# A two-layer attention backbone: a unit's maxes turned by two small matmuls on their way to their row, and output stores entering the queue one batch later

## The chip, the cores and the metric

The kernel runs on one core of one Trainium2 chip. The metric is the device time of one execution in microseconds (us). A core has a matrix engine (TensorE, "PE" in the profile, with its weight loads as "PEld"), a vector engine (VectorE, "DVE"), an engine for functions of one operand (ScalarE, "ACT"), a general engine (GpSimd, "POOL") and SyncE ("SP"), which in this kernel issues every DMA, in the order of the program. PE writes its results to PSUM, from where DVE and ACT read them; everything else lies in SBUF, and DRAM is reached by DMA alone.

## The reference

Two layers over 2048 latent tokens and 256 context tokens of width 1024. In each layer a modulated RMS norm feeds one input projection; its columns go to latent attention (6 heads, "MLA"), to grouped-query attention (6 heads on 2 key heads, "GQA") and to a convolution; their outputs are gated, joined and mapped by one output projection. What bears on the change is the attention:

```python
def block_attention(q, k, v):
    ...
    def one_block(qi):
        s = jnp.einsum('bqgrd,bkgd->bgrqk', qi, k).astype(jnp.float32) * scale
        p = jax.nn.softmax(s, axis=-1).astype(v.dtype)
        return jnp.einsum('bgrqk,bkgv->bqgrv', p, v)
    ...
o_mla = block_attention(q_mla, jnp.concatenate([k_mla, k_mla_c], axis=1),
                        jnp.concatenate([v_mla, v_mla_c], axis=1))
o_gqa = block_attention(q_gqa, jnp.concatenate([k_gqa, k_gqa_c], axis=1),
                        jnp.concatenate([v_gqa, v_gqa_c], axis=1))
```

Latent queries see all 2304 keys; in the first layer the 256 context queries see the context keys alone. In the last layer there are no context queries.

## The kernel before

The program is a row of stages: `projections(0)`, `attention(0)`, `projections(1)` (which ends layer 0 with its output projection and begins layer 1), `attention(1)`, and a last `projections(2)`. The change lies in `attention`. In the profile, attention of layer 0 runs from about 795 to 2070 us, that of layer 1 from about 2935 to 4180 us.

**Units and steps.** A unit is one head and one chunk of queries: chunks 0 to 3 have 512 latent queries, chunk 4 the 256 context queries (layer 0 alone). Heads run in the order 6 to 11 (GQA), then 0 to 5 (MLA). A unit of 512 queries has nine steps, each over 256 keys; a context unit has one. So layer 0 has 6 + 6 heads of 37 steps, layer 1 of 36 steps, and there are 106 units besides the first of each layer, 12 of them context units.

**One step** is a turn of the loop at lines 1605 to 1632. `rows_step` moves the rows of maxes on (below). `s_pair` multiplies the keys with the queries into a PSUM tile `s` (four pairs of matmuls for GQA, five for MLA; the last one adds the row of maxes, which lies in a row of the query tile `qd`), and ACT takes the exponential into a buffer `p`. `next(stream)` does one step of the maxes of a later unit. `sums` adds the buffers on POOL. When enough steps are pending, a batch of them is multiplied with the values (`pv_pair`, PSUM tile `o`): five at a unit's sixth step, four at the next unit's first step (three at a time in the last head). After a unit's last product ACT copies `o` to a tile `e` and SP is given the two stores of it. `finish` makes the sums over keys of two units at a time, copies them to another `e` tile of the same pool of two buffers and gives SP the stores `sm`; their reciprocals are then loaded, computed and stored by tasks of the next stage's planner.

**The maxes.** `max_stream` runs ahead of the units by LEAD steps. For a unit it multiplies queries (as the stationary operand) with a part of the keys into PSUM tiles `m` (a pool of three buffers), eight steps of 512 keys and one of the rest, and DVE reduces each to a column of `mx`, and `mx` to `nm`: 128 partitions x 4 columns, one column for each 128 queries, negated. The matmuls need this as a row of 512 on one partition. Lines 1421 to 1432 do that by DRAM: a step after `nm` is there, the store `nm<-nm` writes it with rows and columns exchanged, and three steps later two loads `qd<-nm` put the row into partitions 32 and 96 of `qd`.

```python
if r[0] == ROW_IN:
    dma(row.rearrange("(j p) -> p j", p=128), r[2].bitcast(F32))
elif r[0] == 0:
    for o, i in m_parts(u, qt[u], row):
        dma(out=o, in_=i)
```

**The order of SP's queue** is that in which `dma` is called. When `max_stream` begins a unit it also calls for the queries of the unit after it (4 DMAs for GQA, 10 for MLA; in chunk 3 those of two units). At the third step of a head's first chunk the next head's keys and values are called for (`load_kv`: `big<-kn` four times, `big<-vm`; for the first MLA head the shared rotary keys as well). The row of the first unit of a layer is made in the projections (`first_unit`, lines 1249 to 1291).

Of the kernel before, what the change touches and what calls it, by code (L numbers as in the profile page):

```python
# [9 lines left out]
F32 = mybir.dt.float32  # L10
F32R = mybir.dt.float32r
# [276 lines left out]
def hybrid_dit(ctx: ExitStack, tc: tile.TileContext, I: dict, out: bass.AP):  # L288
# [1080 lines left out]
    def attention(l, out_proj):  # L1369
        z = scratch[l]  # L1370
        with ExitStack() as ps_:
# [45 lines left out]
                    dma(out=o, in_=i)  # L1417

            rows_due = []

            def rows_step():
                for r in rows_due:
                    r[0] -= 1
                    h, c = u = r[1]
                    row = z.nm[h, c]
                    if r[0] == ROW_IN:
                        dma(row.rearrange("(j p) -> p j", p=128), r[2].bitcast(F32))
                    elif r[0] == 0:
                        for o, i in m_parts(u, qt[u], row):
                            dma(out=o, in_=i)  # L1430
                while rows_due and rows_due[0][0] <= 0:
                    rows_due.pop(0)
# [3 lines left out]
            def max_stream():  # L1436
                for i, u in enumerate(units[1:], 1):
                    h, c = u
                    n = CH[c][1] // 128
                    ahead = i + 2 if c == 3 else i + 1  # L1440
                    while loaded[0] < min(ahead, len(units) - 1):
                        loaded[0] += 1
                        load_q(units[loaded[0]])
                    a, _, cr, _ = qt[u]
                    k = kH[kv_id(h) % 2]
                    mx = mp.tile([128, 4, 6], F32, tag="mx", name="mx")
                    nm = mp.tile([128, 4], F32R, tag="nm", name="nm")
                    ops = [(a, k)] + ([(cr, kR)] if h < MH else [])

                    def banks():  # L1450
                        return [p_m.tile([128, 512], F32, tag="m", name="m") for _ in range(2)]

                    def scores(ps, q, o, w, at=0):
                        for i, (x, y) in enumerate(ops):
                            for e in range(2):
                                r = slice(64 * e, 64 * e + 64)
                                T.matmul(out=ps[e][:, at:at + w], lhsT=x[r, q * 128:q * 128 + 128], rhs=y[r, o:o + w],
                                         start=(i == 0), stop=(i == len(ops) - 1))

                    if c < 4:  # L1460
                        for q in range(n):
                            for i in range(2):
                                ps = banks()
                                scores(ps, q, i * 512, 512)
                                for e in range(2):
                                    V.tensor_reduce(out=mx[:, q, 2 * i + e:2 * i + e + 1], in_=ps[e], op=ALU.max,
                                                    axis=AX.X)
                                yield
                    ps = banks()
                    for q in range(n):  # L1470
                        scores(ps, q, NK - 128, 128, q * 128)
                    for e in range(2):
                        V.tensor_reduce(out=mx[:, 0:n, 4 + e], in_=ps[e][:, 0:n * 128].rearrange("p (q k) -> p q k", k=128),
                                        op=ALU.max, axis=AX.X)
                    V.tensor_reduce(out=nm[:, 0:n], in_=mx[:, 0:n, 0 if c < 4 else 4:6], op=ALU.max, axis=AX.X,
                                    negate=True)
                    rows_due.append([ROW_IN + 1, u, nm[:, 0:n]])
                    yield

            st = {}  # L1480
# [51 lines left out]
            def pv_pair(u, j, t, N, p):  # L1532
# [9 lines left out]
                if j == N - 1:  # L1542
# [6 lines left out]
                    A.activation(out=e1, in_=s["o"], func=AF.Copy)  # L1549
                    r = slice((h % 2) * 64, (h % 2) * 64 + 64)  # L1550
                    o = z.o[h // 2, c]
                    dma(out=o[0, r, :], in_=e1[0:64, :])
                    dma(out=o[1, r, :], in_=e1[64:128, :])
                    fin.append(u)

            fin, ended = [], []

            def finish(last=False):

# [2 lines left out]
                while fin:  # L1562
# [11 lines left out]
                    for e, u in enumerate(us):  # L1574
                        h, c = u
                        fin.remove(u)
                        st.pop(u)
                        dma(out=z.sm[c][h:h + 1, :], in_=e2[64 * e:64 * e + 1, :])
                        out_proj.sch.add(1, out_proj.recip(h, c))

            LAG = 1
            ROW_IN = 3
            LEAD = 16
            qt[units[0]], qt[units[1]] = qall[0:2]
            o, i = kv_parts(z, 0)[-1]
            dma(out=o, in_=i)
# [18 lines left out]
            for u, j, t, N in steps:  # L1605
# [12 lines left out]
                sums(u, j, p, N)  # L1618
                pend.append((u, j, t, N, p))
                if len(pend) >= LAG + batch(pend):  # L1620
                    finish()
                    if pend[0][3] > 1:
                        folds += ended
# [9 lines left out]
            while pend:  # L1633
                finish()
                for x in [pend.pop(0) for _ in range(batch(pend))]:
                    pv_pair(*x)
            folds += ended
            fold_step()
            finish(True)

    stage = [projections(l) for l in range(DEPTH + 1)]
    for _ in stage[0]:
# [89 lines left out]
```

## Time and profile before

| | |
|---|---|
| median of 3 runs | 4395.1 us (4394.66 to 4397.02) |
| the profiled execution | 4391.08 us |
| its span, first to last instruction | 4389.3 us |
| mean granted TensorE clock over the span | 0.946 |
| PE busy | 4012.7 us (91%) |
| DVE busy | 2501.8 us (57%) |
| ACT busy | 1892.2 us (43%) |
| POOL busy | 2478.5 us (56%) |

A row of the waits names the engine that waits, what it waits for, and then us in total, times, and the longest. A row of the timeline has start, duration, engine, line, operation, output <- inputs, shapes and count; in brackets stands how long its engine had been idle, and what ended that. Buffer numbers are left out of names. Almost every instruction has line 159, where a helper records it, so names tell more than lines; SP's DMAs of attention have line 1366, those of the planner line 244. A row of the stretches of time has start and end, length, busy us (and instructions) of PE, PEld, DVE, ACT and POOL, then PE's granted clock, the busy share of the DMA engines, and GB/s.

### The profile page before, as it was taken

To read this page: it belongs to the slowest core of one execution; us is meant where nothing else is said; L and a number is where in the kernel's file an instruction comes from. 1 tells how busy PE (TensorE), PEld (TensorE's weight loads), DVE (VectorE), ACT (ScalarE), POOL (GpSimd) and SP (SyncE) were. 2 spreads that over 40 slices of the span, in tenths; PEclk is the share of its full clock that TensorE was granted. 3 is DMA by queue.
4 is the path that set the end of the run, shared out by engine and by line. 5 is a ranking of instruction groups with operands and counts; after the bars stand their busy time and mean duration, and the time that the engine had idled before them with its cause. 6 is when DMAs were issued, how large, how long until landed. Compare 5 with 4: busy or idle time off the path is not lost.

```text
span 4389.3 us, 61080 instructions
## 1 busy us (share of the span) xinstructions
PE 4012.7 (91%) x22542; PEld 2670.0 (61%) x22542; DVE 2501.8 (57%) x3771; ACT 1892.2 (43%) x2504; POOL 2478.5 (56%) x1277
## 2 busy tenths in 40 slices
PE   7999899998998888898879999999989888888898
PEld 4777467555555555554668777765555555555466
DVE  4643378676665654554435555867667564455463
ACT  4554366444443333333324544644444333333342
POOL 2541254586776566775335324537778666676644
PEclk8999999999999899998989999989999989999899
DMA  5455454434234333333854453552232333333384
GB/s 182 158 160 168 156 163 152 87 43 61 41 48 88 70 69 63 73 76 91 263 173 139 152 194 124 150 135 42 33 60 39 70 71 69 59 65 61 95 259 148
DMA packets 422612, 477.13 MB, mean 109 GB/s; under 512 B 166589, under 2 KB 238982, under 8 KB 422314
## 3 DMA queue, kind: packets, MB, share of 16 engines
q1 hardware_dynamic: 422314, 473.24, 42.2%
q8 instruction: 177, 2.90, 0.4%
q14 instruction: 121, 0.99, 0.1%
HBM read 329.79 MB, written 134.85 MB: 106 GB/s over the span
## 4 chain that ended last, share of the span: by engine, by line
PE 74%; DMA 15%; DVE 5%; SPq 2%; issue 2%; POOL 1%; ACT 1%; POOLq 0%; DVEq 0%; ACTq 0%
PE mm L159 29%; PE s L159 18%; PE o L159 15%; PE m L159 7%; PE aux L159 6%; DMA nm<-nm 4%; DMA qd<-nm 4%; SPq L1366 2%; DVE lent L159 2%; DVE mx L159 2%; DMA lent<-rc 1%; DVE big L159 1%; DMA ql<-qg 1%; DMA ql<-qm 1%; SPq L244 1%
## 5 line engine op out<-in xcount | busy, mean ns | idle before, releaser
L159 DVE TENSOR_REDUCE mx<-m 128x1 f32<-128x512 f32 (+2 forms) x1716 | 1077.3, 681 | 937.3 <-PE m L159 928.6
L159 PE MATMUL mm<-big,wh 128*128 128x512 f32 (+2 forms) x4240 | 1304.7, 391 | 73.1 <-DVE big L159 29.9
L159 POOL TENSOR_TENSOR acc<-acc,p 128x1024 f32<-128x1024 f32 x482 | 1180.6, 2449 | 196.9 <-DVE p L159 94.2
L159 ACT ACTIVATE p<-s 128x1024 f32<-128x1024 f32 (+1 forms) x682 | 694.3, 1019 | 883.6 <-PE s L159 820.9
L159 PEld LDWEIGHTS mm<-big,wh 128*128 128x128 f32 (+1 forms) x4240 | 777.9, 190 | 312.4 <-issue 70.3
L159 PE MATMUL mm<-big,wl 128*128 128x512 f32 (+2 forms) x2120 | 810.5, 382 | 6.4 <-POOL wl L159 6.4
L159 PE MATMUL s<-qh,big 64*128 64x512 f32 (+1 forms) x3504 | 794.6, 413 | 3.8 <-ACT p L159 3.6
L159 POOL TENSOR_TENSOR wl<-wraw,wh 128x1024 fp32r<-128x1024 f32 (+2 forms) x148 | 314.3, 2129 | 724.8 <-ACT wh L159 658.9
L159 PE MATMUL o<-p,big 128*64 128x512 f32 (+1 forms) x2728 | 688.2, 623 | 0.7 <-ACT e L159 0.7
L159 PE MATMUL m<-big,qh 64*128 64x512 f32 (+1 forms) x2304 | 473.9, 367 | 67.7 <-DVE mx L159 66.5
L159 PEld LDWEIGHTS s<-qh,big 64*128 64x128 f32 x3504 | 390.8, 188 | 218.3 <-issue 165.4
L159 PEld LDWEIGHTS mm<-big,wl 128*128 128x128 f32 (+1 forms) x2120 | 401.8, 190 | 87.2 <-POOL wl L159 8.8
L159 PEld LDWEIGHTS o<-p,big 128*64 128x64 f32 x2728 | 198.4, 145 | 389.8 <-issue 384.7
L159 PE MATMUL s<-ql,big 64*128 64x512 f32 (+1 forms) x1752 | 388.9, 394 | 0.0
L159 POOL TENSOR_TENSOR acc<-acc,wraw 128x1024 f32<-128x1024 f32 x142 | 343.6, 2420 | 74.9 <-DVE wraw L159 47.6
L159 PEld LDWEIGHTS m<-big,qh 64*128 64x128 f32 x2304 | 294.6, 192 | 148.0 <-DVE mx L159 112.9
L159 DVE SCALAR_TENSOR_TENSOR aux<-wn,par,aux 128x512 f32<-128x512 f32 (+1 forms) x396 | 259.1, 720 | 120.7 <-ACT aux L159 120.5
L159 PE MATMUL s<-qd,big 33*128 33x512 f32 (+1 forms) x876 | 195.5, 414 | 114.5 <-DMA qd<-nm 114.5
L159 ACT ACTIVATE wraw<-s 128x1024 f32<-128x1024 f32 (+1 forms) x194 | 198.2, 1021 | 198.8 <-PE s L159 184.2
L159 POOL TENSOR_TENSOR acc<-p,p 128x1024 f32<-128x1024 f32 x52 | 125.1, 2405 | 277.5 <-ACT p L159 277.5
L159 POOL TENSOR_TENSOR sb<-sb,sb 128x512 f32<-128x512 f32 (+1 forms) x160 | 193.8, 1219 | 150.3 <-ACT sb L159 127.3
L159 PE MATMUL s<-qd,zm 33*128 33x512 f32 (+1 forms) x876 | 216.6, 407 | 59.4 <-DMA qd<-nm 59.3
(166 smaller groups left out, 4645.0 us busy)
## 6 DMA issues: line engine op xcount, KB each, us to landing
wraw<-in_w_in SPq DMA_DIRECT2D x80, 512.0 KB
o<-e SPq DMA_DIRECT2D x192, 128.0 KB
big<-o SPq DMA_DIRECT2D x96, 256.0 KB
wraw<-in_w_out SPq DMA_DIRECT2D x48, 512.0 KB
sb<-in_w_mod SPq DMA_DIRECT2D x77, 256.0 KB
sb<-in_x SPq DMA_DIRECT2D x58, 256.0 KB
big<-kn SPq DMA_DIRECT2D x48, 288.0 KB
gt<-sb SPq DMA_DIRECT2D x51, 256.0 KB
```

Of the source, the lines that this page charges most:

```text
L159: return f(**kw)
L244: self.queue.dma_start(out=out, in_=in_)
L1366: S.dma_start(out=out, in_=in_)
```

## The change

Four things are altered in `attention`. A new function `turned` takes a unit's `nm` and multiplies each half of its partitions with a 64x64 identity (`turn`, copied once per layer from `ident`): the result, 4 partitions x 64 columns in a PSUM buffer of the pool of `m`, is copied by DVE to `nt`, so that after both halves `nt` has 4 partitions x 128 columns. The row's store then writes four runs of 128. LEAD becomes 17, so that the maxes are ready a step earlier, and `rows_step` calls `turned` in the step that is gained, before `s_pair`; the store and the loads stay at their steps. (The `i` of `if i > 1` is, in chunks 0 to 3, that of the inner loop at line 1462, and so 1; only context units get the 3, that is one step more between the maxes and the turning.) Last, stores of outputs and sums are put on a list `later`, and `stores` sends them ahead of the next batch; `finish` does one group of sums per batch.

```diff
+            turn = mp.tile([128, 64], F32R, name="turn", bufs=1)
+            for e in (0, 64):
+                V.tensor_copy(out=turn[e:e + 64, :], in_=ident[e:e + 64, e:e + 64])
+
+            def turned(nm):
+
+                n = nm.shape[1]
+                nt = mp.tile([4, 128], F32R, tag="nt", name="nt", bufs=1)[0:n, :]
+                for e in range(2):
+                    r = slice(64 * e, 64 * e + 64)
+                    ps = p_m.tile([128, 512], F32, tag="m", name="m")[0:n, 0:64]
+                    T.matmul(out=ps, lhsT=nm[r, :], rhs=turn[r, :], start=True, stop=True)
+                    V.tensor_copy(out=nt[:, r], in_=ps)
+                return nt
...
-                    if r[0] == ROW_IN:
-                        dma(row.rearrange("(j p) -> p j", p=128), r[2].bitcast(F32))
+                    if r[0] == ROW_IN + 1:
+                        r[2] = turned(r[2])
+                    elif r[0] == ROW_IN:
+                        dma(row.rearrange("(j p) -> j p", p=128), r[2].bitcast(F32))
...
-                    rows_due.append([ROW_IN + 1, u, nm[:, 0:n]])
+                    rows_due.append([ROW_IN + (3 if i > 1 else 2), u, nm[:, 0:n]])
...
-                    dma(out=o[0, r, :], in_=e1[0:64, :])
-                    dma(out=o[1, r, :], in_=e1[64:128, :])
+                    later.append((o[0, r, :], e1[0:64, :], None))
+                    later.append((o[1, r, :], e1[64:128, :], None))
...
+            def stores():
+
+                while later:
+                    o, i, u = later.pop(0)
+                    dma(out=o, in_=i)
+                    if u:
+                        out_proj.sch.add(1, out_proj.recip(*u))
...
-                        dma(out=z.sm[c][h:h + 1, :], in_=e2[64 * e:64 * e + 1, :])
-                        out_proj.sch.add(1, out_proj.recip(h, c))
+                        later.append((z.sm[c][h:h + 1, :], e2[64 * e:64 * e + 1, :], u))
+                    if not last:
+                        break
+                    stores()
...
-            LEAD = 16
+            LEAD = 17
...
                 if len(pend) >= LAG + batch(pend):
+                    stores()
                     finish()
```

Where a head begins in layer 0 (MLA, chunk 0), SP's queue had this order before; `o_3` and `o_4` are the outputs of the head before, `nm_1` the row of chunk 1, `qh` to `qd_3` the queries of chunk 3, `kn` and `vm` the next head's keys and values:

```order
L1366 DMA o_3_0_182<-e_11975 64x512 x2
L1366 DMA o_4_0_183<-e_12004 64x256 x2
L1366 DMA nm_1_0_215<-nm 128x4x1
L1366 DMA qh_85<-qm_3_0_128 64x512
L1366 DMA ql_86<-qm_3_0_128 64x512
...
L1366 DMA big_73<-kn_0_114 64x9x128 x4
L1366 DMA big_73<-vm_118 128x18x64
L1366 DMA qd_1_5704<-nm_1_0_215 1x512 x2
```

And it has this order now:

```order
L1366 DMA o_3_0_182<-e_12233 64x512 x2
L1366 DMA qh_85<-qm_3_0_128 64x512
L1366 DMA ql_86<-qm_3_0_128 64x512
...
L1366 DMA nm_1_0_215<-nt 4x128
L1366 DMA big_73<-kn_0_114 64x9x128 x4
L1366 DMA big_73<-vm_118 128x18x64
L1366 DMA qd_1_5704<-nm_1_0_215 1x512 x2
L1366 DMA o_4_0_183<-e_12275 64x256 x2
```

The row's store has moved behind the queries, and the context unit's output behind the keys and the row's loads.

On PE, in layer 0, the end of the maxes of chunk 2 (`qh_83`) now stands ahead of a batch of products with the values, and the two turning matmuls behind that batch:

```order
L159 MATMUL m<-big_73,qh_83 128x128 x8
L159 MATMUL s<-f,ones_f 64x512 x2
L159 MATMUL o<-p_5_5702,big_73 64x512 x2
L159 MATMUL o<-wraw_92,big_73 64x512 x2
L159 MATMUL o<-p_0_5697,big_73 64x512 x2
L159 MATMUL o<-p_1_5698,big_73 64x512 x2
L159 MATMUL m<-turn,nm 4x64 x2
L159 MATMUL s<-qh_81,big_73 128x512 x2
```

Before, that end came a step later, behind the batch, and the scores of the next step followed it at once. For chunk 0 of layer 0 (`qh_79`; PE, in the middle of the chunk 3 before it) nothing stands between:

```order
L159 MATMUL s<-qd_3_5706,zm 128x512 x2
L159 MATMUL m<-big_73,qh_79 128x128 x8
L159 MATMUL m<-turn,nm 4x64 x2
L159 MATMUL s<-qh_85,big_73 128x512 x2
L159 MATMUL s<-ql_86,big_73 128x512 x2
```

Here the turning matmuls, which read `nm`, come directly behind the matmuls from which `nm` is still to be reduced. The same holds for chunk 1, with the two products of the context unit (64x256) between.

More of the change, by code (lines that the diff above doesn't have):

```diff
@@ L1551, in pv_pair @@
                     o = z.o[h // 2, c]
-                    dma(out=o[0, r, :], in_=e1[0:64, :])
-                    dma(out=o[1, r, :], in_=e1[64:128, :])
+                    later.append((o[0, r, :], e1[0:64, :], None))
+                    later.append((o[1, r, :], e1[64:128, :], None))
                     fin.append(u)
-            fin, ended = [], []
+            fin, ended, later = [], [], []
+            def stores():
[4 more added lines that the diff above has]
+                        out_proj.sch.add(1, out_proj.recip(*u))
             def finish(last=False):
@@ L1636, in attention @@
                     pv_pair(*x)
+                stores()
             folds += ended
@@ L1639, in attention @@
             finish(True)
+            stores()
     stage = [projections(l) for l in range(DEPTH + 1)]
```

## The prediction

> **What bounds the kernel now.** I read the page first, then the waits, then the stretches of time, and last the order of time at single places.
>
> ```profile
> span 4389.3 us, 61080 instructions
> PE 74%; DMA 15%; DVE 5%; SPq 2%; issue 2%; POOL 1%; ACT 1%; POOLq 0%; DVEq 0%; ACTq 0%
> PE s L159 <- DMA qd<-nm: 173.7, 47, 13.0
> PE m L159 <- DVE mx L159: 66.5, 29, 7.0
> SPq L1366 <- ACT e L159: 752.5, 151, 18.8
> SPq L1366 <- DMA nm<-nm: 515.1, 95, 10.8
> ```
>
> The first two lines are the page's: TensorE (PE) fills 74% of the chain that ends last, and DMA 15%. The others are waits: total us, times, longest. PE stands 173.7 us for `qd<-nm`, the load that puts a unit's row of maxes into the query tile. It is the largest wait of PE's matmuls in attention; the second, 66.5 us for DVE's max reductions, isn't touched by the change. The last two lines say why the load is late: SP, whose queue issues every DMA in the order of the program, stands 752.5 us before stores of outputs (`e`, written by ACT) and 515.1 us for the store of the row (`nm<-nm`). By stage (heads 6 to 11, then heads 0 to 5, of layer 0 and then of layer 1):
>
> ```profile
> PE s L159 <- DMA qd<-nm: 28.4, 13, 10.9
> PE s L159 <- DMA qd<-nm: 64.4, 12, 8.9
> PE s L159 <- DMA qd<-nm: 29.7, 13, 13.0
> PE s L159 <- DMA qd<-nm: 55.5, 10, 8.0
> ```
>
> Heads 0 to 5 (rows two and four) carry 120 us of it in 22 waits, 5.5 us in the mean. How one comes about, in SP's order of time, with the PE instruction that waits as the last row:
>
> ```profile
> 1596.77 7.71 SPq L1366 DMA_DIRECT2D o<-e  x4
> 1604.76 0.38 SPq L1366 DMA_DIRECT2D nm<-nm  x1
> ...
> 1609.51 0.59 SPq L1366 DMA_DIRECT2D ql<-qm  x1
> 1614.00 0.77 SPq L1366 DMA_DIRECT2D big<-qm  x2
> ...
> 1616.79 2.57 SPq L1366 DMA_DIRECT2D big<-kn  x4
> ...
> 1620.08 5.27 SPq L1366 DMA_DIRECT2D qd<-nm  x2
> 1627.89 1.04 PE L159 MATMUL s<-qd,big 33*128 33x512 f32 x2 [5.98 <-DMA qd<-nm]
> ```
>
> The stores stand at the head of the queue until ACT and DVE are done; the row's store follows at 1604.76; SP then stands again between `ql` (done at 1610.10) and `big` at 1614.00, though that load reads nothing of the row; only then come the next head's keys (`big<-kn`) and, behind them, the row's loads. A PE wait of this length costs more than itself:
>
> ```profile
> 1508.90 1.00 PE L159 MATMUL s<-qd,big 33*128 33x512 f32 x2 [8.43 <-DMA qd<-nm]
> 1500.00:1510.00 10.00, 1.57 (x11) 1.15 (x8) 0.89 (x2) 0.25 (x2) 4.33 (x2) 0.73 0.99 183
> 1510.00:1520.00 10.00, 10.00 (x56) 4.66 (x55) 1.42 (x3) 3.50 (x5) 0.00 (x0) 0.76 0.05 12
> 1545.00:1600.00 55.00, 54.28 (x397) 33.22 (x393) 29.54 (x44) 20.44 (x22) 38.78 (x16) 1.00 0.34 64
> ```
>
> In the last three rows the second number is PE's busy time and the third from the end its granted clock. After the wait of 8.43 us PE is busy for all of 10 us at a clock of 0.76, so (1 - 0.76) x 10 = 2.4 us are lost; with no such wait it runs at 1.00.
>
> **What could be had, measured from above.** ACT copies a unit's output once at its end, so these rows mark the ends of units:
>
> ```profile
> 823.00 0.60 ACT L159 ACTIVATE e<-o 128x512 f32<-128x512 f32 x1 [5.42 <-PE o L159]
> 887.74 0.38 ACT L159 ACTIVATE e<-o 128x256 f32<-128x256 f32 x1
> 972.91 0.38 ACT L159 ACTIVATE e<-o 128x256 f32<-128x256 f32 x1
> 1347.01 0.38 ACT L159 ACTIVATE e<-o 128x256 f32<-128x256 f32 x1
> 1667.79 0.60 ACT L159 ACTIVATE e<-o 128x512 f32<-128x512 f32 x1 [4.17 <-PE o L159]
> 1717.89 0.38 ACT L159 ACTIVATE e<-o 128x256 f32<-128x256 f32 x1
> 2045.29 0.60 ACT L159 ACTIVATE e<-o 128x512 f32<-128x512 f32 x1 [1.29 <-PE o L159]
> 2971.41 0.60 ACT L159 ACTIVATE e<-o 128x512 f32<-128x512 f32 x1 [2.78 <-PE o L159]
> 3012.77 0.60 ACT L159 ACTIVATE e<-o 128x512 f32<-128x512 f32 x1 [2.83 <-PE o L159]
> 3053.93 0.60 ACT L159 ACTIVATE e<-o 128x512 f32<-128x512 f32 x1 [2.84 <-PE o L159]
> 3475.90 0.60 ACT L159 ACTIVATE e<-o 128x512 f32<-128x512 f32 x1 [2.97 <-PE o L159]
> 3674.56 0.60 ACT L159 ACTIVATE e<-o 128x512 f32<-128x512 f32 x1 [4.43 <-PE o L159]
> 3722.36 0.60 ACT L159 ACTIVATE e<-o 128x512 f32<-128x512 f32 x1 [2.94 <-PE o L159]
> 4157.07 0.59 ACT L159 ACTIVATE e<-o 128x512 f32<-128x512 f32 x1
> ```
>
> A good stretch gives the floor of a stage. Layer 0, heads 0 to 5: two units and the context unit take 1717.89 - 1667.79 = 50.1 us, the other two units 47.7, a head 97.8. From 1347.01 to 2045.29 stand five heads and three units, 5 x 97.8 + 72 = 561 of 698 us: 137 too long. Layer 1, the same heads: 3722.36 - 3674.56 = 47.8 for two units, 23 units 550 of 681 us: 131. Heads 6 to 11 of layer 0: a head 972.91 - 887.74 = 85.2; from 823.00 to 1347.01 six heads but their first unit (a fourth of a head, 21) are 490 of 524: 34. Of layer 1: 41.2 for two units, 23 units 473 of 504: 31. Together 333. Without DVE's 66 us, and 13 that I estimate for a slow clock behind them (five long ones x 2.4), **254 us** belong to the row's path. From below: 174 + 24 waits long enough to slow the clock (the 22, and the longest of the other two stages) x 2.4 = **232 us**. I take **245**.
>
> [...]
>
> **The change, part by part.** *The row's store.* It was 512 separate elements, now it is four runs of 128. The trace of before has no store of such a row; the nearest rows are its own store in the old form (longest wait 10.8 us) and the row's loads, also a few long runs, which take SP no more than other DMAs. I take it at nothing, as the loads: SP's 515.1 us lose their cause, and the loads of the row stand three steps behind it as before. At the other end, if it drained as slowly as the old one, that part of the gain, 515 of 515 + 753 us of SP's waits or 41%, wouldn't come.
>
> [...]
>
> *The stores of outputs* enter one batch later, when ACT is long done. What stood behind them moves up. In the rows above the first of them goes out at 1596.77; from there SP now has, in layer 0, two stores, ten query loads and the row's store before the keys. Seven such DMAs (the row's store and six loads) took from 1604.76 to 1610.10, 0.8 us each, so 13 take 10: keys at about 1607 and not 1616.79, 10 us earlier, more than the 5.98 or 8.43 us of wait. For the next unit, twenty query loads now stand ahead of the row's store, but nothing ahead of them waits for ACT, so they run ahead of PE. In layer 1 no store is in the way at all.
>
> *What stays.* The first row of layer 1 is made and stored in the old form:
>
> ```profile
> 2934.43 0.58 PE L159 MATMUL s<-qd,zm 33*128 33x512 f32 x1 [4.59 <-DMA qd<-nm]
> 1076.00:1086.00 10.00, 1.27 (x4) 0.68 (x4) 0.01 (x1) 0.19 (x1) 0.00 (x0) 0.59 0.88 185
> ```
>
> That is 4.6 us. The second row is the load of the first MLA head's keys, which is longest (the 13.0 us above is the same place in layer 1): moved up by some 6 to 8 us, of a wait of 12 or 13 about 5 stay in each layer, with 2.4 of slow clock. Together 4.6 + 15 = **20 us stay**.
>
> *Turning the row.* Each of 106 units adds two matmuls of 64 columns and two DVE copies of 4x64. Eight `m` matmuls of 128 columns take 0.41 us on PE (1141.48 to 1141.89, below), 0.05 each, so two take 0.1 and with their weights 0.12: 106 x 0.12 = 13 us. What counts is PE's wait for the row:
>
> ```profile
> 1141.48 0.68 PE L159 MATMUL m<-big,qh 64*128 64x128 f32 x8
> 1141.89 0.55 PE L159 MATMUL s<-qh,big 64*128 64x512 f32 x2
> 1143.42 0.18 DVE L159 TENSOR_REDUCE nm<-mx 128x4 fp32r<-128x24 f32 x1
> ```
>
> PE goes on at 1141.89, while the row is there at 1143.60; with a hand-over of 0.2 or 0.3 a matmul that needs it would start 2.0 us late, and behind it in PE's queue stands the next step's whole work. In layer 1, and for chunks 2 and 3 of layer 0, a batch of output matmuls (3.6 us) stands between: no wait. In layer 0, chunk 0 has nothing between: 11 x 2.0 = 22. Chunk 1 has the context unit's two short products, 0.6 us: 11 x 1.4 = 15. The context unit is turned a step later, but its second matmul needs a PSUM buffer that DVE still reads, about 0.9: 12 x 0.9 = 11. In all 13 + 22 + 15 + 11 = **61 us**. From both sides: 13 if all is hidden, and 106 x 2.1 = 225 if none is. The DVE copies are below 0.2 us each (the 128x4 reduction takes 0.18), under 42 us of an engine that in the good stretch (1545 to 1600) is busy 29.54 of 55 us: nothing.
>
> **Sum:** 245 - 20 - 61 = 164 us less. The profiled execution took 4391.1 us (span 4389.3), so 4227; the median of the runs shown, 4395.1, is 4.0 higher, so **4231**.
>
> **The rivals.** *Keys stay in front.* The row's loads still stand behind the keys and values in the queue. If these move up only by what the row's old store blocked (1610.10 to 1614.00, 4 of the 10 us), two thirds of the wait at each new head stay: 11 heads x (7.2 in the mean of the two shown + 2.4) and 24 for the two longest are 130, of which 86 stay: 245 - 20 - 86 - 61 = 78 less, **4317**. For it: a DMA share of 0.99 in the wait at 1500; against it: the sum of issue times above.
>
> *Slower: ACT is held by its own copies.* The pool of `e` tiles has two buffers, and every store from them now enters a batch later, so the copy after next may wait for a store that lies behind keys; the exponentials wait behind that copy, and PE for them. At 5 us for each of the 94 full units it would cost 470 against a gain of 164, and from 1.7 us a unit it decides: **4701** at full price. Against it: a unit of 24 us has two batches, so a store has some 10 us until its buffer is asked for again; keys, values and the row's loads together took 11.1 us from 1616.79 to 1627.89, and a store behind them would just fit.
>
> *No change.* The loads of queries (ten or twenty DMAs) come late in the row's place, so that a third of the 245 is gained, and the turning and what stays take it back: 82 - 81, **4394**. Against it: PE's only DMA waits in these four stages are for the row.
>
> **How the numbers follow.** Forecast 0.70; keys in front 0.18; no change 0.05; slower 0.07. The forecast's own ends: 254 with the turning at 13 gives 4174, and if half of DVE's 79 goes too, since its operands come by the same queue, 4134; 232 with turning at 110 gives 4293. The range **4135 to 4325** takes in the first rival; turning at 225 (4395 - 245 + 20 + 225) would be the slower side and is left out with it. A measurement of this kernel tells about 0.2% from no change. Faster 0.89, within 0.2% 0.04, slower 0.07.
>
> **What would show it.** PE's wait for `qd<-nm` falls below 30 us; SP's waits for `e` and for the row's store fall to a tenth; the granted clock in heads 0 to 5 (1.00 in a good stretch) stays above 0.97; a head of this stage in layer 0 takes about 100 us, and not (698 - 72) / 5 = 125. Wrong would be: PE waits for `nm` or `m` in sum over 100 us (turning dearer); waits of 5 us at each new head (first rival); ACT waiting for a DMA before `e` (second).

## The result, and the profile after

The changed kernel takes **4189.6 us** (median of 4 runs, 4183.7 to 4199.2) and the kernel before, beside it, 4396.1 us (4394.7 to 4403.8). The ratio is 0.9529, with a 95% interval of 0.9508 to 0.955. The forecast was 4231, the range 4135 to 4325. The profiled execution took 4188.1 us, 203 us less than that of before, where the working had 164.

The page of the changed kernel, the span, the busy times of its first part and the packets of its second:

```profile
span 4186.4 us, 61644 instructions
PE 3944.2 (94%) x22754; PEld 2679.9 (64%) x22754; DVE 2582.4 (62%) x3987; ACT 1890.2 (45%) x2501; POOL 2488.5 (59%) x1277
DMA packets 370519, 477.16 MB, mean 114 GB/s; under 512 B 114093, under 2 KB 186886, under 8 KB 370218
```

and the same row of packets of the kernel before:

```profile
DMA packets 422612, 477.13 MB, mean 109 GB/s; under 512 B 166589, under 2 KB 238982, under 8 KB 422314
```

The bytes are the same, but 52,496 packets below 512 bytes are gone: 94 rows of 512 and 12 of 256 elements are 51,200, so the old store sent about one packet for each element. PE was idle for 4389.3 - 4012.7 = 377 us before and is for 242 now, 134 less; the other 69 us are PE's busy time, less at a granted clock of 0.965 for 0.946.

PE's waits in attention after the change (us in total, times, longest):

```profile
PE m L159 <- DVE mx L159: 61.1, 51, 4.3
PE m L159 <- DVE nm L159: 28.6, 22, 1.6
PE s L159 <- DMA qd<-nm: 8.6, 4, 3.7
PE m L159 <- DVE nt L159: 7.9, 3, 6.0
```

The wait for the row went from 173.7 us in 47 waits to 8.6 in 4. New are the waits of the turning: for the maxes (`nm`) and, three times, for the copy of a turned half (`nt`). SP's waits, in the same columns:

```profile
SPq L1366 <- DVE nt L159: 466.2, 81, 16.5
SPq L244 <- DVE tiny L159: 402.5, 51, 14.2
SPq L1366 <- ACT e L159: 134.8, 26, 13.3
SPq L1366 <- DMA nm<-nt: 51.2, 54, 2.8
```

SP still stands for hundreds of us, now before the row's store (`nt`) and before the store of reciprocals (`tiny`), but the queue has become early, and PE no longer waits for what it brings. A landed row costs SP 51.2 us in 54 waits, 0.95 each; before it was 515.1 in 95, 5.4 each.

So the other end that the prediction named, a new store that drains as slowly as the old one, did not come: 0.95 us a row against 5.4.

The place of which the prediction showed SP's queue, the third MLA head's start in layer 0, now reads as follows in the order of time (first ACT's copy of a unit's output, then SP):

```profile
1562.32 0.60 ACT L159 ACTIVATE e<-o 128x512 f32<-128x512 f32 x1 [3.82 <-PE o L159]
1562.94 1.09 SPq L1366 DMA_DIRECT2D o<-e  x2
...
1570.79 0.43 SPq L1366 DMA_DIRECT2D nm<-nt  x1
1571.32 2.57 SPq L1366 DMA_DIRECT2D big<-kn  x4
...
1574.65 5.30 SPq L1366 DMA_DIRECT2D qd<-nm  x2
```

From the first store to the keys it is 8.4 us, not 20.0 (1596.77 to 1616.79). The ends of the four stages, by the same rows of ACT as in the prediction:

```profile
823.88 0.60 ACT L159 ACTIVATE e<-o 128x512 f32<-128x512 f32 x1 [2.94 <-PE o L159]
1338.06 0.38 ACT L159 ACTIVATE e<-o 128x256 f32<-128x256 f32 x1 [0.32 <-DMA o<-e]
1977.91 0.60 ACT L159 ACTIVATE e<-o 128x512 f32<-128x512 f32 x1 [1.62 <-PE o L159]
2905.79 0.60 ACT L159 ACTIVATE e<-o 128x512 f32<-128x512 f32 x1 [2.95 <-PE o L159]
3370.70 0.60 ACT L159 ACTIVATE e<-o 128x512 f32<-128x512 f32 x1 [3.35 <-PE o L159]
3954.89 0.60 ACT L159 ACTIVATE e<-o 128x512 f32<-128x512 f32 x1 [1.62 <-PE o L159]
```

The gains are 9.8 us (heads 6 to 11 of layer 0), 58.4 (heads 0 to 5), 39.6 and 97.0 (the same in layer 1), together 204.8; the rest of the program lost 2.

What the turning costs is seen where PE starts it (start, duration, then the idle time ahead and what ended it), here in one head of layer 0:

```profile
1512.02 0.19 PE L159 MATMUL m<-turn,nm 64*4 64x64 f32 x2
1516.31 0.19 PE L159 MATMUL m<-turn,nm 64*2 64x64 f32 x1 [0.75 <-DVE mx L159]
1540.88 0.19 PE L159 MATMUL m<-turn,nm 64*4 64x64 f32 x2 [1.60 <-DVE nm L159]
1566.07 0.19 PE L159 MATMUL m<-turn,nm 64*4 64x64 f32 x2 [1.01 <-DVE nm L159]
```

The first stands behind a batch of output matmuls and waits for nothing; the others are the context unit, chunk 0 and chunk 1.

### The profile page after: what moved, and what is told of

It is laid out like the page before. It is cut to its first block, busy times and chain, and to the rows that moved or that the text cites. A ratio compares the mean times of both kernels' runs of the same rounds, so it can differ in the third digit from the quotient of the medians.

```text
span 4186.4 us, 61644 instructions
## 1 busy us (share of the span) xinstructions
PE 3944.2 (94%) x22754; PEld 2679.9 (64%) x22754; DVE 2582.4 (62%) x3987; ACT 1890.2 (45%) x2501; POOL 2488.5 (59%) x1277
## 5 line engine op out<-in xcount | busy, mean ns | idle before, releaser
L159 PE MATMUL o<-p,big 128*64 128x512 f32 (+1 forms) x2728 | 662.6, 604 | 0.7 <-ACT e L159 0.7
L159 PE MATMUL m<-big,qh 64*128 64x512 f32 (+1 forms) x2304 | 460.7, 368 | 62.9 <-DVE mx L159 52.6
L159 PEld LDWEIGHTS s<-qh,big 64*128 64x128 f32 x3504 | 381.6, 189 | 159.2 <-issue 105.0
L159 POOL TENSOR_TENSOR sb<-sb,sb 128x512 f32<-128x512 f32 (+2 forms) x161 | 193.5, 1210 | 160.5 <-ACT sb L159 148.9
L159 POOL TENSOR_TENSOR acc<-p,p 128x1024 f32<-128x1024 f32 x52 | 125.9, 2421 | 173.7 <-ACT p L159 173.7
L159 PEld LDWEIGHTS s<-ql,big 64*128 64x128 f32 x1752 | 198.8, 190 | 17.8
L159 PE MATMUL s<-qd,zm 33*128 33x512 f32 (+1 forms) x876 | 201.3, 402 | 8.6 <-DMA qd<-nm 8.6
```

What stands on the lines that cost most here:

```text
L159: return f(**kw)
```

## The experiments

My theory was that the two parts of the change act on one path, SP's queue, and that the turning is paid in layer 0 alone. The rivals were that one part alone does it, that LEAD does it, or that the gain comes from elsewhere. The twelve runs were made in four sets, each beside the kernel before, which took 4446 to 4450 us in the median there, not 4396; one experiment below asks what differs between the two occasions. Ratios and differences are therefore formed within the experiments, where the changed kernel took 4192.7.

Stage lengths in us from the first to the last `e<-o` of a stage, as read from ACT's rows. They are those of the profiled execution, whose time can lie up to 8 us off the median beside them. The second column of stages runs to the end of layer 0, two units further than above, and the fourth to the end of layer 1, one unit further. The first unit of a layer lies ahead of its first `e<-o` and so in no column.

| kernel | median us | heads 6–11, layer 0 | heads 0–5, layer 0 | heads 6–11, layer 1 | heads 0–5, layer 1 |
|---|---|---|---|---|---|
| before, first comparison | 4396.1 | 524.0 | 723.8 | 504.5 | 701.5 |
| before, with the experiments | 4448.2 | 540.0 | 734.5 | 524.4 | 710.5 |
| changed | 4192.7 | 512.4 | 657.0 | 464.9 | 603.3 |
| turn, stores at once | 4238.2 | 539.0 | 665.7 | 470.8 | 614.7 |
| late stores, no turn | 4277.8 | 522.6 | 690.3 | 474.9 | 639.9 |
| LEAD 17 alone | 4457.9 | 538.4 | 734.1 | 542.2 | 704.5 |
| turn done twice | 4253.4 | 527.0 | 681.0 | 475.6 | 616.3 |
| turn behind the scores | 4168.4 | 504.6 | 647.6 | 478.0 | 601.9 |
| only outputs late | 4162.2 | 509.6 | 644.9 | 465.5 | 597.1 |
| all three edits | 4142.8 | 499.5 | 636.2 | 473.0 | 600.3 |

### One part at a time

The turn with stores at once:

```diff
-                    later.append((o[0, r, :], e1[0:64, :], None))
-                    later.append((o[1, r, :], e1[64:128, :], None))
+                    dma(out=o[0, r, :], in_=e1[0:64, :])
+                    dma(out=o[1, r, :], in_=e1[64:128, :])
...
-                        later.append((z.sm[c][h:h + 1, :], e2[64 * e:64 * e + 1, :], u))
-                    if not last:
-                        break
-                    stores()
+                        dma(out=z.sm[c][h:h + 1, :], in_=e2[64 * e:64 * e + 1, :])
+                        out_proj.sch.add(1, out_proj.recip(h, c))
```

> The changed kernel with the stores of outputs and sums issued at once again, as before; the turning, the row's store of four runs and LEAD 17 stay. Theory (both parts act on one path, SP's queue, and each alone frees a part of it): 4250 to 4330 us; SP's wait for e is back above 500 us, its wait for a row's store is gone; PE still waits 60 to 110 us for qd. Rival 1 (the slow store of the row was all): 4190, and PE waits under 20 us for qd. Rival 2 (the stores at the head of the queue were all): about 4396 plus the turning's 30 to 60, 4430 to 4455.

Late stores (and LEAD 17) without the turn:

```diff
-                    if r[0] == ROW_IN + 1:
-                        r[2] = turned(r[2])
-                    elif r[0] == ROW_IN:
-                        dma(row.rearrange("(j p) -> j p", p=128), r[2].bitcast(F32))
+                    if r[0] == ROW_IN:
+                        dma(row.rearrange("(j p) -> p j", p=128), r[2].bitcast(F32))
```

> The changed kernel without the turning: the row is stored element by element from nm again, at the same step; late stores and LEAD 17 stay. Theory (one path, two parts): 4230 to 4320 us; SP's wait for a row's store is back above 300 us, its wait for e stays below 150; PE waits 40 to 110 us for qd. Rival 1 (the slow store was all): about 4396. Rival 2 (the stores at the head were all, and the turning only costs): 4130 to 4160, below the changed kernel, with PE's wait for qd under 20 us.

And the changed kernel beside them:

> The changed kernel itself, beside the others on this chip, where the kernel before took 4447.7 us and the turn with immediate stores 4238.2 us. Theory (once the maxes are turned, the late stores bring nothing that can be measured): 0.953 of the kernel before, 4230 to 4247 us, the same as with immediate stores. Rival (the late stores bring a share of their own): 4195 to 4222 us, which would be 0.943 to 0.949.

Measured: the turn alone 4238.2 us, ratio 0.953 (0.9515 to 0.9544); late stores alone 4277.8, 0.9612 (0.9596 to 0.9628); both 4192.7, 0.9429 (0.941 to 0.9448). Alone they bring about 210 and 170 us, together 255 or 256: the parts overlap, as the theory had it. But the turn alone is 12 us below the theory's interval, and PE's wait for the row there (19.5 us, below) is the first rival's and not the theory's 60 to 110: the faster store does more by itself than I thought. And the changed kernel came out just below the interval of the third expectation's rival, so that its theory falls: late stores are worth some 45 us beside the turn. PE's and SP's waits with stores at once:

```profile
PE m L159 <- DVE nt L159: 28.6, 9, 5.6
PE s L159 <- DMA qd<-nm: 19.5, 10, 5.1
SPq L1366 <- ACT e L159: 1181.9, 154, 26.6
```

and with late stores, but the row in elements:

```profile
PE m L159 <- DVE mx L159: 99.3, 54, 7.9
PE s L159 <- DMA qd<-nm: 48.9, 14, 9.8
SPq L1366 <- DMA nm<-nm: 637.6, 85, 10.7
```

With the old row, SP stands as long for its landing as it ever did, but only 48.9 of PE's 199.8 us (the kernel before, on this occasion) remain. With the turn and stores at once, SP stands 1181.9 us for `e`, and 19.5 remain. Either edit makes the queue early enough in most places.

Part of the 45 us was not expected. PE's wait for `nt` is 28.6 us and not 8, and the trace puts it down to one buffer. In the third head of this kernel (SP, DVE, PE, in that order):

```profile
1028.74 1.11 SPq L1366 DMA_DIRECT2D o<-e  x2
1029.89 1.55 SPq L244 DMA_DIRECT2D rc<-tiny  x3
1031.54 0.28 SPq L1366 DMA_DIRECT2D nm<-nt  x1
1035.47 0.34 DVE L159 CAST nt<-m 2x64 fp32r<-2x64 f32 x2 [3.54 <-DMA nm<-nt]
1035.73 0.79 PE L159 MATMUL m<-big,qh 64*128 64x512 f32 x1 [2.92 <-DVE nt L159]
```

`nt` has a single buffer, and two turns follow each other closely at a context unit. With stores at once, the first row's store waits in the queue behind the store of `e` and three stores of reciprocals (`rc`), and then has to land; so the second turn's copy can't be written, its PSUM buffer isn't freed, and PE stands 2.92 us. In the whole kernel DVE waits 35.3 us in nine waits for the store of `nt`; with late stores it has no such wait. A second buffer of `nt` would test this alone; it wasn't tried.

### LEAD alone

```diff
-            LEAD = 16
+            LEAD = 17
```

> The kernel before with LEAD 17 for 16 and nothing else: every max, row and key load stands one step earlier on SP. Theory (the keys are late because SP's queue is held, and a step earlier is one step less late): PE waited for keys 47 times before; at most 2.4 us less at each is 113 us, and since the row still writes element by element and SP still waits for e, half of that: 4370 to 4420 us. Rival (the lead alone does nothing, the queue is as full as before): 4435 to 4455 us. Second rival (the lead alone is most of what the late stores' kernel gained, 170 us): 4270 to 4330 us.

Measured: 4457.9 us, ratio 1.0022 (1.0008 to 1.0035). The first rival holds (the time is 3 us above its interval), and the theory is wrong: PE's and SP's waits

```profile
PE s L159 <- DMA qd<-nm: 177.3, 48, 14.1
SPq L1366 <- ACT e L159: 854.3, 153, 21.4
```

show the key wait 22 us smaller and SP's wait for `e` 110 us larger than in the same kernel with LEAD 16 (199.8 and 744.8). A row called for earlier waits in the same queue; what the late stores brought is not LEAD's.

### The turn's place and its price

The turn behind the step's score matmuls:

```diff
-                    if r[0] == ROW_IN + 1:
-                        r[2] = turned(r[2])
-                    elif r[0] == ROW_IN:
+                    if r[0] == ROW_IN:
...
+            def turn_step():
+                for r in rows_due:
+                    if r[0] == ROW_IN + 1:
+                        r[2] = turned(r[2])
...
                 p = s_pair(u, j, t)
+                turn_step()
```

> The changed kernel, with the two turning matmuls issued behind the scores of their step and not ahead of them (still ahead of the step's maxes); the store of the row stays at its step. If the turning's price is PE's wait for nm and for a PSUM buffer (28.6 us and some 9 us in the changed kernel's waits, all in layer 0): these go, 4150 to 4165 us. Rival (the price lies in the added instructions and hand-overs, or DVE only hands the wait on to the next maxes): 4180 to 4195, and the waits of PE's m matmuls for DVE grow by what goes.

The same with stores at once, as in the first experiment:

> The turn behind the step's score matmuls, with the stores issued at once as in the kernel before. With late stores this took 4168.4 us. Theory (with four rows stored in one piece SP's queue has slack, so that waiting for e costs nothing): 4160 to 4185 us. Rival (with the turn's own waits gone, the wait for e on SP shows again): 4190 to 4215 us, with PE's wait for qd at 20 us or more in sum.

And each turn done twice, the first result overwritten unread:

```diff
                     if r[0] == ROW_IN + 1:
+                        turned(r[2])
                         r[2] = turned(r[2])
```

> The changed kernel with each of the 106 turns done twice, the first result overwritten unread: four matmuls and four copies for two. This measures the price of a turn at its place. By matmul time alone 106 x 2 x 0.19 = 40 us at most; each further pair also waits once or twice for the buffer that the copy before it reads, 0.75 us as the context units' turns do now. Theory (a turn costs by its waits and by the clock behind them): 80 to 190 us more than the changed kernel beside it. Rival (PE takes the turn beside other waits, and it costs what the prediction took for its matmuls, 0.12 us each time): 10 to 45 us more.

Measured: behind the scores 4168.4 us (0.9368, 0.9354 to 0.9382), 24 less than the changed kernel and 3 above the theory's interval. The waits go as the theory had it: PE's for `nm` fall from 28.6 us to 5.5, and those for `mx` fall too, from 62.5 to 41.0, so DVE doesn't hand the wait on. But the time isn't shown to follow from them. Of the 24.4 us between the two profiled executions only 5.5 lie in the four stages; 8.4 lie between the layers and behind the second one, and 10.5 ahead of the first `e<-o`, in the first unit of layer 0. There the granted clock differs (rows of the changed kernel, of this one, and of the last kernel below, with all three edits):

```profile
796.00:806.00 10.00, 8.75 (x43) 5.97 (x39) 6.99 (x12) 3.07 (x3) 7.03 (x4) 0.50 1.22 204
796.00:806.00 10.00, 8.70 (x50) 4.33 (x51) 7.42 (x15) 2.43 (x3) 7.67 (x4) 1.00 1.25 202
796.00:806.00 10.00, 9.12 (x42) 6.20 (x42) 6.92 (x12) 2.69 (x4) 7.10 (x3) 0.50 1.23 204
```

PE is about as busy in all three, at a clock of 0.50, 1.00 and 0.50. The last has its turn behind the scores as well, so the place of the turn doesn't settle this clock; what does is open.

With stores at once the turn behind the scores takes 4236.2 us (0.9523, 0.9502 to 0.9543): the place of the turn is then worth nothing (4238.2 ahead of the scores), and PE still waits 32.6 us for `nt` in 21 waits. That is outside both intervals; the theory that the queue has slack falls, and the rival named the wrong wait (17.4 us for `qd`). Done twice, the turn costs 61 us more (4253.4; 0.9562, 0.9543 to 0.9582), 0.57 each, above the rival's 10 to 45 and below the theory's 80.

The stages tell where the turn is paid. Behind the scores, layer 0 gains 7.8 and 9.4 us and heads 6 to 11 of layer 1 lose 13.1: a unit there takes 20.1 or 20.9 us and not 19.6 or 20.3. In heads 0 to 5 of layer 1 units lose as much (24.0 and 24.9 us), and the stage is 1.4 us shorter only because one unit of the last head took 26.8 us and not 39.9, which wasn't explained. In layer 1 the turn ahead of the scores is free: units take 19.6 and 20.3 us (heads 6 to 11) and 23.4 and 24.2 (heads 0 to 5) with it and, in the kernel without a turn, 19.6 and 20.3, and 23.4 and 24.3. It lies in a gap that PE's weight loads have anyhow behind a batch of output matmuls: without a turn this gap stands 222 times ahead of score loads (169.7 us in all, put down to issue), with it 142 times there (109.7 us) and 67 times ahead of the turn's loads (55.2 us). Behind the scores the gap stands ahead of score loads again (229 times, 172.5 us), and the turn with its two matmuls of 0.19 us comes on top of it. That is the likely reason for the half a us, not a tested one. A turn behind the scores in layer 0 alone suggests itself; it wasn't tried.

LEAD set back to 16 with the turn behind the scores:

```diff
-            LEAD = 17
+            LEAD = 16
```

> The turn behind the step's score matmuls with late stores (4168.4 us), with LEAD back at 16: every row and its keys come one step later, some 2 us. Theory (the row's path is now far shorter than its lead, and a step less is still enough): 4160 to 4180 us, PE's wait for qd under 15 us in sum. Rival (the lead's step is needed, since the row now waits a step for its turn): 4200 to 4280 us, with PE's wait for qd at 40 us or more.

Measured: 4234.9 us (0.9518, 0.9494 to 0.9542), the rival's time without the rival's cause. PE's waits:

```profile
PE m L159 <- DVE nm L159: 46.1, 90, 2.7
PE s L159 <- DMA qd<-nm: 12.1, 4, 4.8
```

The row comes in time (12.1 us), but nearly every turn now waits for its maxes, 0.5 us in the mean: LEAD shifts the maxes against the units' batches, and with it what stands between the last max and the turn. The loss is spread over the units: in layer 1 they take 20.8 and 21.6 us (heads 6 to 11) and 24.6 and 25.5 (heads 0 to 5), 0.6 or 0.7 more than with LEAD 17, which for 94 full units is 56 to 66 us.

One transpose and one copy for a turn's two matmuls and two copies:

```diff
-                for e in range(2):
-                    r = slice(64 * e, 64 * e + 64)
-                    ps = p_m.tile([128, 512], F32, tag="m", name="m")[0:n, 0:64]
-                    T.matmul(out=ps, lhsT=nm[r, :], rhs=turn[r, :], start=True, stop=True)
-                    V.tensor_copy(out=nt[:, r], in_=ps)
+                ps = p_m.tile([128, 512], F32, tag="m", name="m")[0:n, 0:128]
+                T.transpose(out=ps, in_=nm.bitcast(F32), identity=ident)
+                V.tensor_copy(out=nt, in_=ps)
```

> The turn behind the scores with late stores (4168.4 us), with one transpose of all 128 partitions by the identity and one copy for a turn's two matmuls and two copies: 106 copies of 0.2 us fewer on DVE, 106 m buffers fewer. Done twice, a turn of two matmuls and two copies cost 61 us in all (0.57 us each). Theory (a turn behind the scores still costs by its second buffer and second copy): 4135 to 4160 us. Rival (behind the scores a turn is hidden but for its matmuls, and the transpose takes as long on PE as two matmuls): 4162 to 4175 us.

Measured: 4161.0 us (4154.1 to 4163.4), against 4168.4 (4159.2 to 4169.9) in another set of runs: 7.5 us less in the median, with executions that overlap, just below the rival's interval and just above the theory's. The time doesn't tell them apart. In the profiled executions the four stages are 13.4 us shorter together and the rest of the program is 4.1 longer.

### Outputs late, sums at once

The changed kernel with the second half of the first experiment's diff alone (the sums' stores at once, all finished groups in one batch).

> The changed kernel with only the attention outputs stored late; the sums are stored at once, and all groups that are done are finished in one batch, as before. Beside it on this chip the changed kernel took 4192.7 us and the one with all stores at once 4238.2 us. Theory (it is SP's wait for ACT's copy e, 1182 us with stores at once and 135 us with late ones, that holds the rows and keys behind it): 4185 to 4205 us. Rival (the sums' store and the groups finished together hold SP just as long): 4220 to 4240 us.

Measured: 4162.2 us (0.9359, 0.9337 to 0.9381), 30 less than the changed kernel and better than either side expected. SP's waits:

```profile
SPq L1366 <- ACT e L159: 719.6, 62, 18.1
SPq L244 <- DVE tiny L159: 117.4, 44, 5.7
```

SP again stands 720 us for `e`, and PE's wait for the row stays what it was (9.8 us; 9.7 in the changed kernel): a total of SP's waits doesn't say whether anyone waits for SP. So neither side's cause holds. Late sums are worse than early ones; the edit brings back both the stores at once and the groups finished together, and these two weren't told apart. In the profiled executions the kernel is 31 us shorter, 20 of them in the four stages and 8 between the layers. DVE shows where a part of it comes from. In the changed kernel, at a head's first chunk in layer 1 (start, duration, engine, operation, shapes):

```profile
3581.86 2.53 DVE L159 TENSOR_TENSOR lent<-lent,lent 128x512 f32<-128x512 f32 x1
3584.42 2.73 DVE L159 TENSOR_TENSOR lent<-big 128x512 f32<-128x512 f32 x1
...
3589.88 2.83 DVE L159 TENSOR_TENSOR lent<-lent,lent 128x512 f32<-128x512 f32 x1
3592.63 1.28 DVE L159 TENSOR_REDUCE mx<-m 128x1 f32<-128x512 f32 x2
3593.36 0.66 PE L159 MATMUL m<-big,qh 64*128 64x512 f32 x1 [3.46 <-DVE mx L159]
```

and around the same head's start with the sums stored at once:

```profile
3556.86 1.95 DVE L159 TENSOR_TENSOR lent<-lent,lent 128x512 f32<-128x512 f32 x1
3558.84 0.69 DVE L159 TENSOR_TENSOR lent<-big 128x512 f32<-128x512 f32 x1
3559.57 0.69 DVE L159 TENSOR_TENSOR lent<-lent,lent 128x512 f32<-128x512 f32 x1
3561.57 2.40 POOL L159 TENSOR_TENSOR acc<-p,p 128x1024 f32<-128x1024 f32 x1 [3.31 <-ACT p L159]
```

These three operations prepare the output projection and can start when the sums' reciprocals are back. With early sums the first meets the end of a POOL addition, and the other two fall into a gap of POOL (idle for 3.31 us until 3561.57) and take 0.69 us each; with late sums they fall beside POOL's additions, take 2.5 to 2.8 us each, hold up the max reductions, and PE waits 3.46 us. That unit takes 29.8 us instead of 24.6, and so does the same unit two heads later: 10 us in layer 1. The same two units of layer 0 are together 6.5 us shorter with early sums. The rest of the 31 us wasn't told apart.

Up to 2.83 us is about the 0.69 of the operation and most of a POOL addition of 2.40. Why the operation takes that long there, no row shows.

### The kernel before, profiled beside the experiments

> The kernel before, profiled beside the others on this chip: its time is 4448 us here in 17 runs, and was 4396 us on the chip of the first comparison, while the changed kernel took 4190 us there and 4193 us here. Theory (the element-by-element row is what differs: SP's wait until a row has landed was 515 us in 95 waits, and PE's wait for keys 174 us): both sums are larger here, PE's wait for keys by 25 to 60 us, and the stages outside the units are as long as they were. Rival (the chip's clock or its other work is slower): the stages outside the units are longer too, in proportion.

Measured: 4449.5 us in one run. The waits, against 173.7 and 515.1:

```profile
PE s L159 <- DMA qd<-nm: 199.8, 54, 13.6
SPq L1366 <- DMA nm<-nm: 541.2, 88, 12.5
```

The four stages of attention are longer by 16, 11, 20 and 9 us, 56 of the 58 us of span; the rest of the program adds 3. The theory holds as far as place and wait go. A landing costs SP 6.2 us instead of 5.4. Whether that is the chip or the moment isn't known. Since the changed kernel took 4189.6 and 4192.7, what varied most likely lies in what the change removed: its gain was 206 us the one time and 255 the other.

### The best of it together

Outputs late, sums at once, the turn behind the scores with one transpose and one copy:

> The changed kernel with the turn behind the scores, one transpose and one copy for a turn, and the sums stored at once with all groups finished together; only the attention outputs are stored late. On this chip the changed kernel took 4192.7 us, and the edits alone 4168.4 us (turn behind the scores), 4161.0 us (that with one copy) and 4162.2 us (only outputs late). Theory (they mend different waits: the turn's behind the maxes, and DVE's adds that fall beside POOL's in a head's first chunk, 5.4 us in every second head of layer 1): the gains add, 4120 to 4145 us. Rival (both gain by moving DVE's folds away from the maxes, and the second finds little left): 4150 to 4170 us.

Measured: **4142.8 us** (0.9311, 0.9289 to 0.9332), the theory's upper end: 50 less than the changed kernel, where the gains of the separate edits, 30 and 32, are 62. The executions form two groups, 4139.6 to 4142.8 and 4150.8 to 4152.3 us, and the profiled one, with the clock of 0.50 in its first unit, is of the second. PE's wait for `mx` falls to 38.3 us in 33 waits, that for `nm` to 5.6.

## Why the prediction was right, point by point

**The bound and the mechanism** were right. PE's wait for `qd<-nm` was to fall below 30 us; it is 8.6. The keys were to move up by 10 us against the unit's end, and the queue from first store to keys shrank by 11.6. That both holders of the queue count is shown by the first two experiments.

**The size by stage.** Sharing the 245 as the stages stood above their floors (DVE's 79 taken half and half from heads 0 to 5 of the layers), and taking off the turning and what stays, the forecast of 164 has -2 and 66 us for layer 0's two stages and 20 and 86 for layer 1's (less 4.6 for the first row, ahead of them). What stays is taken off in the stages of heads 6 to 11, since the first MLA head's keys are loaded in head 9. Measured are 9.8 and 58.4, 39.6 and 97.0. Layer 0 is as forecast only in its sum (68 and 64), and that is luck: one stage is 12 better and the other 8 worse. **Layer 1 is 31 us better**, most of the 39 by which the forecast fell short. Five terms were mis-sized:

- *The floor of heads 6 to 11 in layer 1.* I took 41.2 us for two units, but that stretch still held small waits for the row. They take 19.6 + 20.3 = 39.9; for 23 units that is 15 us.
- *What stays.* At head 9, 5 us of wait and 2.4 of slow clock were to stay in each layer; PE waits 2.8 us there in layer 0 and 1.2 in layer 1. The first row of layer 1 costs the 4.6 us that it was put at. Together that is the 8.6 us, and not 20.
- *Turning in layer 1.* Its matmuls, 47 of the 106 turns at 0.12 or about 6 us (a turn's pair takes 0.19 in the trace), cost nothing there, as units with and without the turn show.
- *Turning in layer 0.* It is 10 us cheaper (next paragraph but one).
- *The late sums,* put at nothing. In heads 0 to 5 of layer 0, the one stage below its forecast, the kernel with early sums is 12.1 us shorter.

**DVE's 66 us** were left at nothing: it is 61.1 now, and in heads 0 to 5 of layer 1 it fell from

```profile
PE m L159 <- DVE mx L159: 29.6, 9, 7.0
```

to

```profile
PE m L159 <- DVE mx L159: 21.2, 11, 4.3
```

With the 3 us of turning that aren't paid there, these 8.4 us are about the 11 by which that stage beat its forecast; why DVE's maxes came earlier was not tested apart.

**Turning the row.** The three places came where they were put, each cheaper: 1.60 us (2.0), 1.01 (1.4), 0.75 (0.9); 11 x 1.60 + 11 x 1.01 is the 28.6 of the waits for `nm`, and with 12 x 0.75 it is 38 and not 48. The hand-over, put at 0.2 or 0.3 us by my estimate, which no run shows, was too dear: PE starts the turn shown with the result at 1540.88, 0.05 after DVE's `nm` ends at 1540.83. Missed were two things. The copies to `nt` were put at nothing, but with one buffer they tie the turn to the queue: 6.0 us once in the changed kernel, 28.6 with stores at once. And that the turn's price depends on what stands ahead of it on PE also in layer 1, where it is free in one place and half a us a unit in the other, wasn't weighed.

**Two readings** in the prediction were off, without weight. Its four rows by stage add up to 178.0 us and not 173.7, because a wait of 4.2 us in head 11 of layer 0 stands in the first two; between the ends of the stages used here heads 0 to 5 wait 114.5 us in 20 waits, not 120 in 22. And five slow clocks of 2.4 us are 12, not 13.

**The late stores** were right for the outputs, wrong for the sums with their groups finished one by one. The step "what stood behind them moves up" looked at SP's queue alone; that the sums' stores start the planner's work on DVE, and that this would meet POOL's additions, was not in it. With early sums the kernel is 30 us shorter, of which the units read in the trace of layer 1 make 10. Two of the signs came only in part: a clean head of layer 0 takes 102.2 us as forecast (about 100), but every second one 108 to 110, and the clock in heads 0 to 5 is 0.96 in layer 0 and 0.98 in layer 1, not above 0.97 in both. And SP's wait for `e` fell to 18%, not a tenth; the kernel with early sums, where it is back at 720 us, shows that this sign says little.

**The rivals.** No wait of 5 us for the row remains at a new head: keys don't stay in front. The slower case had ACT waiting for stores of its own `e`: that is 1.3 us in four waits, and all of ACT's waits for a DMA ahead of `e` are 20.1 us in 16, against a price of 470. The wait does exist: with late stores and the old row ACT stood 49.1 us in ten waits, up to 9.7 us, for stores of sums (`sm<-e`), and PE 8.3 us for `e`.

## What to carry to other kernels

In a queue that issues in order, ask of each wait not how long it is but what stands behind it and when that is needed: SP waits more than 700 us for `e` in the kernel before and in the one with early sums, and PE waits 173.7 us for its rows in the first and 9.8 in the second. Two edits that clear the same queue needn't add up (about 210 and 170 us alone, 255 together here), and one can still be needed for the other's buffers. When a store moves, follow what starts once it has landed: the tasks that it releases may fall beside work that holds them up (DVE's additions took 0.69 us in one place and up to 2.83 in the other). And before a gain is put down to an edit, look in which stretch of the program it lies: of 24 us, 19 lay outside the stages in which the edit was read.

## What was not expected of the hardware

- The old store of a row, 512 elements, goes as about one packet per element (52,496 packets below 512 bytes fewer for 51,200 elements), and SP's wait for its landing was 5.4 us on one occasion and 6.2 on the other, with the kernel's time 52 us apart; the same bytes in four runs cost 0.95.
- DVE's additions `lent` of 128x512 take 0.69 us in a gap of POOL's and 2.5 to 2.8 us beside its additions.
- Two small matmuls directly behind a batch of output matmuls cost no time that a unit's length shows (in heads 6 to 11 of layer 1 19.6 and 20.3 us with and without them), and half a us per unit behind score matmuls (20.1 and 20.9).
- In the first unit of layer 0 the granted clock of the changed kernel stays at 0.50 in the row from 796 to 806 us, with PE busy for 8.41 of 10 us in the first profile and 8.75 in the second; the kernel before is at 1.00 in the same stretch, with PE busy for 9.50.
